# Sliding the operand window of a down projection: one row tile per visit in a ring of eight, and another order at the start of the up stage

## The chip, the cores and the metric

The kernel runs on one core of one Trainium2 chip. The metric is the time of one execution in microseconds on the device; lower is better. Before the change three runs took 2235.82, 2242.28 and 2243.55 us, median 2242.28 us.

## The reference

One layer of a decoder with two token groups, 512 prompt tokens and 8 x 4 sample tokens, 544 in all. A mixer (retention and sliding-window attention) comes first; then the feed-forward part, which is what the change touches:

```
def conv_ffn(h, conv_buf, ffn_norm_w, w_up, conv_w, conv_b, w_down):
    hn = rmsnorm(h, ffn_norm_w)
    up = jnp.einsum('btd,df->btf', hn, w_up)          # 2048 -> 2 x 5632
    g, u = jnp.split(up, 2, axis=-1)
    gp = jnp.concatenate([conv_buf.astype(g.dtype), g], axis=1)
    gc = conv_b + sum(gp[:, j:j + T] * conv_w[j] for j in range(CONV_W))
    y = jnp.einsum('btf,fd->btd', jax.nn.silu(gc) * u, w_down)   # 5632 -> 2048
    return y, gp[:, -(CONV_W - 1):]
...
hp = hp + mixer_output(ro, rg, so, ret_gn_w[l], w_o[l], hp.dtype)
f, cbuf_p = conv_ffn(hp, zbuf, ffn_norm_w[l], w_up[l], conv_w[l], conv_b[l], w_down[l])
hp = hp + f
```

All inputs are float32.

## The kernel before

**Precision.** A float32 product is made of three matmuls of a reduced float32 type: each operand is split into `hi` (a rounded copy, written by ACT) and `lo` (the rest, a subtraction on DVE), and hi x lo, lo x hi and hi x hi are summed (`split`, L149).

**Tiling.** The 544 tokens are two halves of 272 columns (256 prompt, 16 sample tokens), index u. Up and down projection both work on 2 x 2 blocks (two halves of tokens, two halves of the other sides) with seven products in place of eight, named `b11 t1 t2 b21 t3 b22 t4` in the order in which `unit` (L1104) makes them. A product (`product`, L1092) takes a weight block, 128 columns by up to eight row tiles of 128 rows; ACT and DVE split it (`uhi`, `ulo`; three buffers each), and PE runs 3 matmuls of 128 x 272 for each row tile against the seven moving operands in `xop`: `X_hi/X_lo` for b11, t1 and t2, `A_hi/A_lo` for the others. Each of the seven has eight slots, one for each row tile. Some weight blocks are sums on DVE (`usum`, L1132, L1135, L1146, and in place L1142).

**Up stage.** 44 visits (`up_pair`, f = 0 to 43), each with the seven products at eight row tiles. Behind each come the norm factor, the convolution, the gate (`joined`, `conv`, `gated`), and for every second visit `blocks` (L1196), which makes the seven operands of the down projection for one of its 22 row tiles j and writes them to DRAM (`hx_keep[0..6]`, by DMAs that POOL issues).

**Down stage.** The 22 row tiles do not fit into the eight slots, so they are taken in three chunks, `chunks = ((0, 8), (8, 7), (15, 7))` (L1217). For every chunk there are eight visits (`down_pair`, mp = 0 to 7, 256 output columns each): 24 visits. Results of the first two chunks are added into `x1_keep` in DRAM (`keep_y`), those of the last are finished and written out (`finish_y`, `emit_y`). Before a chunk, all seven operands are filled again: `fill(c, name)` (L1219) reads all row tiles of the chunk from `hx_keep` into the `lo` slots (one DMA issued by POOL) and splits them in place, four row tiles at a time. The fill of a product's operand is written behind that product in the last visit before the chunk:

```
1276  unit(load, (y[:, 1, 0], y[:, 1, 1]), todo, joined, sign=-1.0, behind=fills(c + 1) if mp == 7 else {})
1281  todo = up_pair(f, todo, behind=fills(0) if f == FT - 1 else {})
```

**Start of the up stage.** The stage before it, the second part of the output projection (L1026 to L1042), makes x1 one column block at a time (i = 0 to 15), and `build_x` makes the operands from two of them. After it come the four splits of L1043 to L1045 into `A_hi/A_lo` slots 0 to 7 (operands b21 and t4), then the sum of squares is turned into the norm factor by a matmul (`rstd_ffn`, L1078), then `unit` of f = 0 loads its weights (`uraw`, 7 buffers: 3 in pool `ua`, 4 in pool `ub`). Pool `ua` lies where the pools of the output projection (`wp`: raw, whi, wlo; `tb1`: x1, sq2, t1k) were.

**Order.** A scheduling layer turns the written order into one instruction stream for each engine; an engine runs its stream in order, and semaphores hold an instruction until what it needs is done. Weights come by DMAs that SP issues, `hx_keep` and `x1_keep` by DMAs that POOL issues.

## Time and profile before

| | us |
|---|---|
| median of three runs | 2242.28 |
| profiled execution | 2239.99 |
| its span, first to last instruction | 2238.2 |
| PE busy in the span | 2176.6 (97%) |
| DVE busy | 1630.1 (73%) |
| ACT busy | 1010.7 (45%) |
| POOL busy | 291.9 (13%) |

The mean granted clock of TensorE over the span is 0.986 of full speed. A busy share is an average over stages: the up stage runs from about 760 to 1715 us, the down stage from there to the end. The times in rows below count from the span's start.

### The profile page before, as it was taken

Reading aid. Unit: us, or ns where it says so; the run is one execution under the profiler, and the core shown is the slowest. Engines: PE = TensorE matmul, PEld = TensorE weight load, DVE = VectorE, ACT = ScalarE, POOL = GpSimd, SP = SyncE. Lnnn points to the kernel's source line nnn. Section 1 sums busy time; section 2 is a strip of 40 time slices with the busy share of each in tenths; the row PEclk is TensorE's granted clock in tenths of the full one; section 3 lists DMA queues with packets and bytes.
Section 4 is the critical chain, followed back from the end, with each engine's and each line's share of the span. In section 5 each row is a group of like instructions: output and inputs, shape, how many; then the busy total and the mean of one; then the engine's idle time right before and its main releaser. Section 6 shows DMA issues by size and latency. Waiting matters only on the chain.

```text
span 2238.2 us, 42004 instructions
## 1 busy us (share of the span) xinstructions
PE 2176.6 (97%) x17159; PEld 2139.1 (96%) x17159; DVE 1630.1 (73%) x2457; ACT 1010.7 (45%) x1612; POOL 291.9 (13%) x463
## 2 busy tenths in 40 slices
PE   7999999999999799999999999999998999898998
PEld 7999999999999799999999999999998999898998
DVE  5555557875437778888888888888888767767775
ACT  5122235566215544444444444444445445445444
POOL 1000000000003212122122122122122101001000
PEclk8999999999999899999999999999998999999999
DMA  9333343324644343343443443434436656557553
GB/s 289 100 97 94 87 88 77 82 67 120 130 115 136 112 124 114 113 145 107 121 137 113 124 125 116 133 114 126 124 116 224 149 128 194 139 131 221 140 150 98
DMA packets 452656, 286.52 MB, mean 128 GB/s; under 512 B 46320, under 2 KB 430640, under 8 KB 452080
## 3 DMA queue, kind: packets, MB, share of 16 engines
q1 hardware_dynamic: 433376, 222.16, 36.6%
q0 software_dynamic: 19088, 61.68, 9.1%
q8 instruction: 134, 2.20, 0.4%
q14 instruction: 58, 0.48, 0.1%
HBM read 231.38 MB, written 47.67 MB: 125 GB/s over the span
## 4 chain that ended last, share of the span: by engine, by line
PE 64%; issue 18%; DVE 9%; DMA 6%; POOL 2%; ACT 1%; SPq 1%; DVEq 0%; POOLq 0%; ACTq 0%
PE acc L174 17%; PE acc L178 9%; PE bx L1100 7%; PE bx L1099 6%; PE bx L1102 6%; PE zy L1099 5%; PE zy L1100 5%; PE zy L1102 4%; DMA uraw<-in_w_up_dram 3%; DVE ulo L151 3%; DMA A_lo<-hx_keep 1%; POOL x_keep L1267 1%; DVE cv L1186 1%; DVE us L1191 1%; PE sm L686 1%
## 5 line engine op out<-in xcount | busy, mean ns | idle before, releaser
L151 DVE TENSOR_TENSOR ulo<-uraw,uhi 128x1024 fp32r<-128x1024 f32 (+1 forms) x272 | 322.1, 1188 | 87.3 <-ACT uhi L150 87.0
L150 ACT CAST uhi<-uraw 128x1024 fp32r<-128x1024 f32 (+1 forms) x272 | 278.2, 1023 | 108.6 <-issue 72.2
L150 ACT CAST uhi<-usum 128x1024 fp32r<-128x1024 f32 (+1 forms) x204 | 209.3, 1026 | 227.0 <-DVE usum L1135 123.4
L1100 PE MATMUL bx<-X_hi,ulo 128*128 128x272 f32 x1056 | 277.2, 294 | 11.6 <-DVE ulo L151 11.4
L174 PE MATMUL acc<-A_lo,whi 128*128 128x272 f32 x1344 | 286.2, 294 | 1.4 <-DVE A_lo L290 0.8
L1099 PE MATMUL bx<-X_lo,uhi 128*128 128x272 f32 x1056 | 275.2, 291 | 9.7 <-ACT uhi L150 9.7
L174 PE MATMUL acc<-A_hi,wlo 128*128 128x272 f32 x1344 | 280.6, 290 | 0.0
L151 DVE TENSOR_TENSOR ulo<-usum,uhi 128x1024 fp32r<-128x1024 f32 (+1 forms) x204 | 242.6, 1189 | 47.3 <-ACT uhi L150 47.3
L1099 PE MATMUL bx<-A_lo,uhi 128*128 128x272 f32 x1056 | 271.0, 289 | 4.7 <-ACT us L1122 2.2
L1099 PE MATMUL zy<-A_lo,uhi 128*128 128x272 f32 x1056 | 272.5, 290 | 1.3 <-ACT p L1124 0.5
L1100 PE MATMUL zy<-A_hi,ulo 128*128 128x272 f32 x1056 | 271.4, 289 | 0.6 <-DVE ulo L151 0.6
L1100 PE MATMUL bx<-A_hi,ulo 128*128 128x272 f32 x1056 | 270.1, 287 | 0.0
L150 ACT CAST whi<-raw 128x1024 fp32r<-128x1024 f32 x100 | 104.8, 1048 | 279.4 <-PE acc L178 234.2
L174 PEld LDWEIGHTS acc<-A_lo,whi 128*128 128x128 f32 x1344 | 211.8, 189 | 7.9 <-issue 4.2
L1100 PEld LDWEIGHTS bx<-X_hi,ulo 128*128 128x128 f32 x1056 | 202.3, 192 | 16.5 <-DVE ulo L151 16.2
L174 PEld LDWEIGHTS acc<-A_hi,wlo 128*128 128x128 f32 x1344 | 211.9, 189 | 0.8
L1099 PEld LDWEIGHTS bx<-X_lo,uhi 128*128 128x128 f32 x1056 | 201.9, 191 | 11.0 <-ACT uhi L150 10.9
L1099 PEld LDWEIGHTS bx<-A_lo,uhi 128*128 128x128 f32 x1056 | 199.2, 189 | 5.8 <-ACT us L1122 2.4
L1099 PEld LDWEIGHTS zy<-A_lo,uhi 128*128 128x128 f32 x1056 | 199.7, 189 | 2.5 <-ACT p L1124 1.1
L1100 PEld LDWEIGHTS zy<-A_hi,ulo 128*128 128x128 f32 x1056 | 199.6, 189 | 0.8 <-DVE ulo L151 0.8
L1100 PEld LDWEIGHTS bx<-A_hi,ulo 128*128 128x128 f32 x1056 | 198.9, 188 | 0.0
L178 PE MATMUL acc<-A_hi,whi 128*128 128x272 f32 x1344 | 187.6, 290 | 0.0
(437 smaller groups left out, 4256.6 us busy)
## 6 DMA issues: line engine op xcount, KB each, us to landing
uraw<-in_w_up_dram SPq DMA_DIRECT2D x176, 512.0 KB
uraw<-in_w_down_dram SPq DMA_DIRECT2D x64, 448.0 KB
raw<-in_w_in_dram SPq DMA_DIRECT2D x52, 512.0 KB
uraw<-in_w_down_dram SPq DMA_DIRECT2D x32, 512.0 KB
hx_keep<-us POOLq DMA_DIRECT2D x88, 136.0 KB, 2.0
hx_keep<-tt POOLq DMA_DIRECT2D x66, 136.0 KB, 4.8
x_keep<-us POOLq DMA_DIRECT2D x32, 272.0 KB, 5.1
raw<-in_w_in_dram SPq DMA_DIRECT2D x32, 256.0 KB
```

The costliest lines, as they stand in the source:

```text
L150: act.copy(out=hi, in_=src)
L151: eng.tensor_tensor(out=lo, in0=src, in1=hi.bitcast(F32), op=sub)
L174: pe.matmul(acc[:, u, :HC], lhsT=w, rhs=x[:, u, :], start=(first and i == 0 and w is wh), stop=False)
L178: pe.matmul(acc[:, u, :HC], lhsT=wh, rhs=xh[:, u, :], start=False, stop=(last and i == n - 1))
L686: pe.matmul(po[:, 256 * kv:256 * kv + 256], lhsT=vS[:, n if n == 0 else n - 1 + kb, kv, :], rhs=t[:, kb, :], start=(j == 0), stop=(j == le ...
L1099: pe.matmul(bank, lhsT=hi[:, k], rhs=xl[:, k], start=(first and k == 0), stop=False, skip_group_check=True)
L1100: pe.matmul(bank, lhsT=lo[:, k], rhs=xh[:, k], start=False, stop=False, skip_group_check=True)
L1102: pe.matmul(bank, lhsT=hi[:, k], rhs=xh[:, k], start=False, stop=(k == n - 1), skip_group_check=True)
L1186: dve.scalar_tensor_tensor(out=cva, in0=g[:, 0:560], scalar=w0[:, f:f + 1], in1=cva, op0=mult, op1=add)
L1191: dve.tensor_tensor(out=us, in0=us, in1=rstd_bc, op=mult)
L1267: sth(out=x1_keep[2 * mp + i], in_=y[:, i], accum_op=add)
```

## The change

The three chunks go. The down stage still has 24 visits, in three rounds of eight, but the range of row tiles that a visit takes now moves on by one tile from visit to visit: visit v uses tiles t0 = start + v % 8 up to t0 + n, with (start, n) = (0, 6), (6, 8), (14, 8), row tiles counted modulo 22. For each output column block the three rounds still cover all 22 tiles once. A tile t lies in slot t % 8 of each operand. In each visit each operand gets one new tile (`next_fills`): its DMA is written behind that product, its split ("convert") four products later, behind that product's own weight split. Before the first visit six tiles for each operand are filled (`first_fills`): DMAs behind the products of f = 43, the split of b11's operand behind f = 43, those of the six others in visit 0, one product ahead of their use. A visit's weight block has six or eight row tiles instead of eight or seven; a range that passes tile 21 takes two DMAs.

At the start of the up stage the weight block of f = 0's first product is loaded and split already in the output projection's last pass, in its pools; b11 of f = 0 is written ahead of the last four splits of x and ahead of the norm factor's matmul; pools `ua` and `ub` open later (behind b11 and behind t1's split). f = 0 thus loads that block twice, once for b11 and once for the sums.

The transposes for the convolution's last rows (`conv_rows`) are written two visits later, and may not stand ahead of the last matmul written before them.

The diff, cut to its core:

```diff
@@ -1026,6 +1026,8 @@
         acc = half_project(m, 1, A_hi[:, 0:8], A_lo[:, 0:8])
+        if i == KT - 1:
+            first_w = stage_half(cols_of(w_up[0], 0), 0)
...
@@ -1040,19 +1042,25 @@
-    for u in range(2):
-        for k in range(0, 8, 4):
-            split(A_hi[:, k:k + 4, u], A_lo[:, k:k + 4, u], C[:, k + 8:k + 12, u])
-    tst.close()
-    wst.close()
     ost.close()
...
+    def open_ua():
+        tst.close()
+        wst.close()
+        ua.append(ust.enter_context(tc.tile_pool(name="ua", bufs=1, reuse_waits="tile")))
+
+    def last_x():
+
+        for u in range(2):
+            for k in range(0, 8, 4):
+                split(A_hi[:, k:k + 4, u], A_lo[:, k:k + 4, u], C[:, k + 8:k + 12, u])
+        cst.close()
+        ub.append(ust2.enter_context(tc.tile_pool(name="ub", bufs=1, side="right", reuse_waits="tile")))
...
@@ -1072,14 +1080,15 @@
-            pe.matmul(pm[:, :HC], lhsT=onesD, rhs=ssq[:, u, :], start=True, stop=True)
+            with tc.issue_after(ups["mm"].ins):
+                pe.matmul(pm[:, :HC], lhsT=onesD, rhs=ssq[:, u, :], start=True, stop=True)
...
@@ -1089,19 +1098,28 @@
+            ups["split"] = split(hi, lo, w)
+        for part in between:
+            part()
+        n = hi.shape[1]
         xh, xl = xop[x]
         for ks in parts or (range(n),):
             for k in ks:
-                pe.matmul(bank, lhsT=hi[:, k], rhs=xl[:, k], start=(first and k == 0), stop=False, skip_group_check=True)
-                pe.matmul(bank, lhsT=lo[:, k], rhs=xh[:, k], start=False, stop=False, skip_group_check=True)
+                q = (at + k) % 8
+                pe.matmul(bank, lhsT=hi[:, k], rhs=xl[:, q], start=(first and k == 0), stop=False, skip_group_check=True)
+                pe.matmul(bank, lhsT=lo[:, k], rhs=xh[:, q], start=False, stop=False, skip_group_check=True)
...
@@ -1123,34 +1140,40 @@
-        a11, a21, a22 = load(0, 0), load(1, 0), load(1, 1)
-        prod(bx, a11, "b11", True, False)
+        if first_w is None:
+            a11, a21, a22 = load(0, 0), load(1, 0), load(1, 1)
+            prod(bx, a11, "b11", True)
+        else:
+            prod(bx, first_w, "b11", True)
+            open_ua()
+            a11, a21, a22 = load(0, 0), load(1, 0), load(1, 1)
...
@@ -1208,31 +1234,65 @@
-    chunks = ((0, 8), (8, 7), (15, 7))
-
-    def fill(c, name):
-        def go():
-            j0, n = chunks[c]
...
+    rounds = ((0, 6), (6, 8), (14, 8))
+    late = {}
+
+    def window(v):
+
+        t0, n = rounds[v // 8]
+        return t0 + v % 8, n
+
+    def fill(t, n, name):
+
+        hi, lo = (a[:, t % 8:t % 8 + n] for a in xop[name])
+        raw = lo.bitcast(F32)
+
+        def load():
+            sth(out=raw, in_=hx_keep[order7.index(name)][:, t % FJ:t % FJ + n])
+
+        def convert():
+
+            a, d = ups["split"]
+            with tc.issue_after(a.ins), tc.issue_after(d.ins):
+                for h in range(0, n, 4):
+                    p = slice(h, min(h + 4, n))
+                    if name == "t2":
...
+                    else:
+                        split(hi[:, p], lo[:, p], raw[:, p])
+        return load, convert
+
+    def first_fills():
+
+        steps = [fill(0, rounds[0][1], name) for name in order7]
+        now = {name: step[0] for name, step in zip(order7, steps)}
+        for i in range(1, 7):
+            late[0, order7[i - 1]] = [steps[i][1]]
+
+        def end():
+            steps[6][0]()
+            steps[0][1]()
+
+        now["t4"] = end
+        return now
+
+    def next_fills(v):
+
+        if v == 23:
+            return {}
+        now = {}
+        for i, name in enumerate(order7):
+            now[name], convert = fill(v + 6, 1, name)
+            late.setdefault((v + (i + 4) // 7, order7[(i + 4) % 7]), []).append(convert)
+        return now
...
@@ -1273,12 +1338,14 @@
-        unit(load, (y[:, 1, 0], y[:, 1, 1]), todo, joined, sign=-1.0, behind=fills(c + 1) if mp == 7 else {})
+        behind = next_fills(v)
+        within = {name: late.get((v, name), ()) for name in order7}
+        unit(load, (y[:, 1, 0], y[:, 1, 1]), todo, joined, sign=-1.0, behind=behind, within=within, at=t0)
...
     for f in range(FT):
-        todo = up_pair(f, todo, behind=fills(0) if f == FT - 1 else {})
+        todo = up_pair(f, todo, behind={"t1": last_x} if f == 0 else first_fills() if f == FT - 1 else {})
...
-    for c in range(len(chunks)):
-        for mp in range(8):
-            if c == 0 and 1 <= mp < 6:
-                todo[3] = [conv_rows(mp - 1)]
-            todo = down_pair(c, mp, todo)
+    for v in range(24):
+        if 2 <= v < 7:
+            todo[3] = [conv_rows(v - 2)]
+        todo = down_pair(v, todo)
```

In these pieces of the engines' streams rows are in order; `x4` counts equal instructions.

DVE where the up stage begins, before the change: the output projection's last splits, the norm factor (g, cv, rstd_bc) and f = 0's first products (ulo, usum).

```order
L1018 TENSOR_TENSOR t1k<-C 128x272
L151 TENSOR_TENSOR A_lo<-C,A_hi 128x4x272
L151 TENSOR_TENSOR X_lo<-t1k,X_hi 128x272
L1011 SCALAR_TENSOR_TENSOR X_lo<-C,X_hi 128x272
L151 TENSOR_TENSOR A_lo<-C,A_hi 128x272
L1023 TENSOR_TENSOR C<-C 128x272
L1083 TENSOR_SCALAR g<-sm 128x272 x2
L151 TENSOR_TENSOR A_lo<-C,A_hi 128x4x272
L151 TENSOR_TENSOR ulo<-uraw,uhi 128x1024
L195 SCALAR_TENSOR_TENSOR cv<-g,rstd_bc 128x544
L1132 TENSOR_TENSOR usum<-uraw 128x1024
```

The same place after the change:

```order
L1018 TENSOR_TENSOR t1k<-C 128x272
L151 TENSOR_TENSOR A_lo<-C,A_hi 128x4x272
L151 TENSOR_TENSOR X_lo<-t1k,X_hi 128x272
L1011 SCALAR_TENSOR_TENSOR X_lo<-C,X_hi 128x272
L151 TENSOR_TENSOR A_lo<-C,A_hi 128x272
L1023 TENSOR_TENSOR C<-C 128x272
L151 TENSOR_TENSOR A_lo<-C,A_hi 128x4x272
L1156 TENSOR_TENSOR usum<-uraw 128x1024
L1166 TENSOR_TENSOR uraw<-uraw 128x1024
L151 TENSOR_TENSOR ulo<-usum,uhi 128x1024
L151 TENSOR_TENSOR ulo<-uraw,uhi 128x1024
L1159 TENSOR_TENSOR usum<-usum,uraw 128x1024
```

b11's weight split and the norm factor are gone from this place; the first weight work is now the sum for t1 (L1156).

SP's stream at the same place before the change, with the semaphores that each DMA waits for (DMASW and DMAHW: DMAs issued by POOL and by SP):

```order
L950 DMA raw<-in_w_o_dram 128x8x128 [waits DMAHW7_49,DVE_49]
L165 DMA uraw<-in_w_up_dram 128x8x128 [waits DMAHW2_49,DMAHW0_49,DVE_49]
L165 DMA uraw<-in_w_up_dram 128x8x128 [waits DMAHW1_49,PE_49]
L165 DMA uraw<-in_w_up_dram 128x8x128
L165 DMA uraw<-in_w_up_dram 128x8x128 [waits DVE_49]
```

And after it:

```order
L950 DMA raw<-in_w_o_dram 128x8x128 [waits DMAHW7_49,DVE_49]
L165 DMA raw<-in_w_up_dram 128x8x128 [waits DMAHW0_49,DVE_49]
L165 DMA uraw<-in_w_up_dram 128x8x128 [waits DMASW4_49,DMASW3_49,DMASW5_49,DMASW2_49,DMASW6_49,DMASW1_49,DMASW7_49,DMASW0_49,DVE_49]
L165 DMA uraw<-in_w_up_dram 128x8x128 [waits DMAHW3_49,DMAHW2_49]
L165 DMA uraw<-in_w_up_dram 128x8x128 [waits Pool_49]
L165 DMA uraw<-in_w_up_dram 128x8x128 [waits DVE_49,PE_49]
```

The load of b11's block comes first and lies in `raw`. The first `uraw` load behind it now lies on tb1's tiles: its DMASW waits are the POOL DMAs that read x1, its DVE wait is X_lo<-t1k of the last `build_x`.

DVE at the first fill, before the change: f = 43's last weight splits (ulo), then fills of eight tiles, two instructions of four tiles for each operand.

```order
L1146 TENSOR_TENSOR usum<-usum,uraw 128x1024
L151 TENSOR_TENSOR ulo<-uraw,uhi 128x1024
L151 TENSOR_TENSOR X_lo<-X_lo,X_hi 128x1088 x2
L151 TENSOR_TENSOR ulo<-usum,uhi 128x1024
L151 TENSOR_TENSOR X_lo<-X_lo,X_hi 128x1088 x2
L151 TENSOR_TENSOR ulo<-uraw,uhi 128x1024
L1229 SCALAR_TENSOR_TENSOR X_lo<-X_lo,X_hi 128x1088 x2
L1145 TENSOR_TENSOR us<-us,p_19260 128x272
L151 TENSOR_TENSOR A_lo<-A_lo,A_hi 128x4x272 x2
```

The same place after the change:

```order
L1166 TENSOR_TENSOR uraw<-uraw 128x768
L151 TENSOR_TENSOR ulo<-uraw,uhi 128x1024
L151 TENSOR_TENSOR ulo<-usum,uhi 128x1024
L151 TENSOR_TENSOR ulo<-uraw,uhi 128x1024
L151 TENSOR_TENSOR X_lo<-X_lo,X_hi 128x1088
L151 TENSOR_TENSOR X_lo<-X_lo,X_hi 128x544
L1170 TENSOR_TENSOR us<-us,p_19296 128x272
L151 TENSOR_TENSOR ulo<-uraw,uhi 128x768
L151 TENSOR_TENSOR X_lo<-X_lo,X_hi 128x1088
L1197 TENSOR_TENSOR g<-zy,tu 128x512
```

f = 43's weight splits now stand ahead of all fills; from t1's fill on they stand between the splits of visit 0 (128x768, six tiles).

POOL in the middle of the down stage, before the change: sums into x1_keep for a whole chunk, then seven fills, then sums again.

```order
L1267 DMA x_keep<-us 128x544 x14
L1224 DMA X_lo<-hx_keep 128x1904 x3
L1224 DMA A_lo<-hx_keep 128x7x272 x4
L1267 DMA x_keep<-us 128x544 x16
```

After the change, one visit:

```order
L1332 DMA x_keep<-us 128x544
L1258 DMA X_lo<-hx_keep 128x272
L1332 DMA x_keep<-us 128x544
L1258 DMA X_lo<-hx_keep 128x272 x2
L1258 DMA A_lo<-hx_keep 128x272 x4
```

The two sums of a visit now stand among seven loads of one tile.

## Rows read from the trace of the kernel before

**Rows 1.** The page: busy time of each engine and its share of the span.

```profile
PE 2176.6 (97%) x17159; PEld 2139.1 (96%) x17159; DVE 1630.1 (73%) x2457; ACT 1010.7 (45%) x1612; POOL 291.9 (13%) x463
```

**Rows 2.** PE's waits from 700 us on: total us, times, longest.

```profile
PE bx L1100 <- DVE ulo L151: 11.4, 13, 4.9
PE bx L1099 <- ACT uhi L150: 9.7, 3, 5.5
```

**Rows 3.** Stretches: length, busy us of PE PEld DVE ACT POOL, PEclk, DMA share, GB/s.

```profile
900.00:1680.00 780.00, 776.22 (x6164) 772.83 (x6163) 663.35 (x829) 367.85 (x515) 162.89 (x278) 1.00 0.41 122
1700.42:1734.63 34.21, 24.77 (x154) 23.96 (x153) 30.63 (x32) 22.47 (x27) 7.23 (x11) 0.80 0.76 256
1745.00:1880.00 135.00, 134.98 (x1079) 134.70 (x1077) 92.09 (x86) 55.81 (x78) 12.21 (x15) 1.00 0.55 126
2100.00:2220.00 120.00, 119.97 (x957) 118.50 (x957) 84.93 (x91) 57.72 (x98) 9.53 (x13) 1.00 0.50 137
```

**Rows 4.** Timeline of PE at the three fills: start, us, instruction.

```profile
1700.42 0.29 PE L1099 MATMUL zy<-A_lo,uhi 128*128 128x272 f32 x1
...
1734.63 0.28 PE L1099 MATMUL bx<-X_lo,uhi 128*128 128x272 f32 x1
...
1894.67 1.16 PE L1102 MATMUL zy<-A_hi,uhi 128*128 128x272 f32 x8
...
1922.50 1.04 PE L1102 MATMUL zy<-A_hi,uhi 128*128 128x272 f32 x7
...
2051.43 1.04 PE L1102 MATMUL zy<-A_hi,uhi 128*128 128x272 f32 x7
...
2086.29 1.03 PE L1102 MATMUL bx<-A_hi,uhi 128*128 128x272 f32 x7
```

**Rows 5.** Timeline of PE where the up stage begins.

```profile
757.52 2.17 PE L178 MATMUL acc<-A_hi,whi 128*128 128x272 f32 x16
...
773.82 0.43 PE L1099 MATMUL bx<-X_lo,uhi 128*128 128x272 f32 x1
...
774.27 0.43 PE L1099 MATMUL bx<-X_lo,uhi 128*128 128x272 f32 x1
...
781.94 0.28 PE L1099 MATMUL bx<-X_lo,uhi 128*128 128x272 f32 x1
```

**Rows 6.** Timeline of DVE at the same place.

```profile
763.25 1.46 DVE L1017 TENSOR_TENSOR C<-C 128x272 f32<-128x272 f32 x1
...
766.54 0.43 DVE L151 TENSOR_TENSOR X_lo<-t1k,X_hi 128x272 fp32r<-128x272 f32 x1
...
769.25 1.29 DVE L151 TENSOR_TENSOR A_lo<-C,A_hi 128x1088 fp32r<-128x1088 f32 x1 [0.52 <-ACT A_hi L150]
```

**Rows 7.** DMA from 740 to 800 us in 40 slices of 1.5 us.

```profile
GB/s 0 0 142 182 211 0 174 12 11 0 180 6 0 19 241 324 298 3 0 0 0 199 329 290 290 275 15 21 291 37 34 254 298 125 4 256 89 5 0 0
```

**Rows 8.** DVE by form from 1740 us: count, busy us, mean ns, idle before.

```profile
L151 DVE TENSOR_TENSOR ulo<-uraw,uhi 128x1024 fp32r<-128x1024 f32 x29 | 35.2, 1222 | 12.4 <-ACT uhi L150 12.3
...
L1145 DVE TENSOR_TENSOR us<-us,p 128x272 f32<-128x272 f32 x24 | 10.6, 442 | 20.8 <-ACT us L1124 20.8
L151 DVE TENSOR_TENSOR A_lo<-A_lo,A_hi 128x1088 fp32r<-128x1088 f32 x8 | 10.3, 1289 | 3.4 <-ACT A_hi L150 3.2
```

**Rows 9.** Timeline of DVE at the first fill.

```profile
1693.67 1.22 DVE L1135 TENSOR_TENSOR usum<-usum,uraw 128x1024 f32<-128x1024 f32 x1
...
1700.28 1.21 DVE L151 TENSOR_TENSOR ulo<-uraw,uhi 128x1024 fp32r<-128x1024 f32 x1
```

**Rows 10.** Timeline of POOL, start of the up stage and first fill.

```profile
763.08 1.32 POOL L1042 TENSOR_TENSOR rstd_bc<-rstd_bc,sq 128x544 f32<-128x544 f32 x1 [0.56 <-ACT sq L1041]
...
1693.76 0.54 POOL L1224 DMA_DIRECT2D X_lo<-hx_keep  x1
```

**Rows 11.** DMA issues, 1690 to 1735 us: count, KB each, us to landing.

```profile
A_lo<-hx_keep POOLq DMA_DIRECT2D x4, 1088.0 KB, 10.4
...
hx_keep<-us POOLq DMA_DIRECT2D x3, 136.0 KB, 2.0
```

More of the change, by code (lines that the diff above doesn't have):

```diff
@@ L1090, in b44, with product @@
         return a.rearrange("p u (b t) -> p u b t", t=4)
-    def product(bank, w, x, first, last, parts=None):
-        n = w.shape[1]
-        hi, lo = new_hi()[:, :n], new_lo()[:, :n]
-        split(hi, lo, w)
+    def product(bank, w, x, first, parts=None, between=(), at=0):
+        if isinstance(w, tuple):
+            hi, lo = w
+        else:
+            hi, lo = new_hi()[:, :w.shape[1]], new_lo()[:, :w.shape[1]]
+            ups["split"] = split(hi, lo, w)
+        for part in between:
+            part()
+        n = hi.shape[1]
         xh, xl = xop[x]
@@ L1111, in prod @@
         def prod(*a):
-            product(*a, parts=parts)
+            product(*a, parts=parts, between=within.get(a[2], ()), at=at)
             if a[2] in behind:
@@ L1209, in blocks @@
             sth(out=hx_keep[1][:, j], in_=tt[:, 2])
-        unit(load_up(f), (us[:, 0], us[:, 1]), todo, joined, behind=behind, parts=None if f else (range(7), range(7, 8)))
+        unit(load_up(f), result, todo, joined, behind=behind, parts=None if f else (range(7), range(7, 8)), first_w=None if f else first_w)
         return {1: [conv], 6: [gated], 2: [blocks] if f % 2 else []}
@@ L1234, in fills @@
-    def fills(c):
-        return {name: fill(c, name) for name in order7} if c < len(chunks) else {}
+    FJ = FT // 2
+    rounds = ((0, 6), (6, 8), (14, 8))
[14 more added lines that the diff above has]
+                    if name == "t2":
+                        act.activation(out=hi[:, p], in_=raw[:, p], func=AF.Copy, scale=-1.0)
+                        dve.scalar_tensor_tensor(out=lo[:, p], in0=raw[:, p], scalar=-1.0, in1=hi[:, p].bitcast(F32), op0=mult, op1=sub)
+                    else:
+                        split(hi[:, p], lo[:, p], raw[:, p])
+        return load, convert
@@ L1249, in emit_y, with down_pair @@
         ld(out=y_sample.rearrange("b t d -> (b t) d")[:, 128 * m:128 * m + 128], in_=ys)
-    def down_pair(c, mp, todo):
-        j0, n = chunks[c]
-        last = c == len(chunks) - 1
+    def down_pair(v, todo):
+        t0, n = window(v)
+        mp = v % 8
+        last = v >= 16
         y = new_us()
@@ L1258, in load @@
             col = 128 * (2 * mp + i)
-            ld(out=raw, in_=wd[256 * j0:256 * (j0 + n), col:col + 128].rearrange("(j two p) c -> two p j c", two=2, p=128)[q])
+            j0 = t0 % FJ
+            for k0, k1 in ((0, min(n, FJ - j0)), (FJ - j0, n)):
+                if k0 < k1:
+                    j = (t0 + k0) % FJ
+                    ld(out=raw[:, k0:k1], in_=wd[256 * j:256 * (j + k1 - k0), col:col + 128].rearrange("(j two p) c -> two p j c", two=2, p=128)[q])
             return raw
```

61 lines of the change are left out of this document (27 added, 34 removed).

## The prediction

> **What bounds the kernel now.** I read the page first: PE is busy for 97% of the span [rows 1], so only the stretches in which it is not are worth looking at. The list of PE's waits after the attention part comes next; its two longest groups are matmuls that wait for DVE's or ACT's split of a weight block, each with few waits of up to 5 us [rows 2]. The timeline of PE says where: at the start of the up stage and at the three fills of the down stage's operands. Elsewhere PE is full: 776.2 of 780 us in the up stage, and all but 0.1 us in two stretches of the down stage [rows 3]. That also gives the yardstick: 776.22 us for 6164 matmuls is 0.126 us each, 3.02 us for a product of eight row tiles, 2.64 us for seven, 2.27 us for six.
>
> What each place loses, as time between two matmuls less the matmuls between them:
> - First fill [rows 4]: 1700.42 (f = 43's b21 begins) to 1734.63 (visit 0's t2 begins) is 34.2 us. Six products of eight tiles need 18.1 us and eight transposes about 1.1 us. Lost: 15.0 us. DVE is busy for 30.6 of these 34.2 us and the mean granted clock is 0.80 [rows 3], so this stretch goes at DVE's pace, and PE runs part of it at the lower of its two levels.
> - Second fill [rows 4]: 1894.67 to 1922.50 is 27.8 us. Between these rows lie 8 + 24 + 3 x 21 + 14 = 109 matmuls, 13.7 us. Lost: 14.1 us.
> - Third fill [rows 4]: 2051.43 to 2086.29 is 34.9 us; 7 + 7 x 21 + 14 = 168 matmuls, 21.1 us. Lost: 13.8 us.
> - Start of the up stage [rows 5]: 757.52 to 781.94 is 24.4 us; 64 matmuls (8.1 us) and four of the norm factor (0.5 us). Lost: 15.8 us.
>
> **Part 1: second and third fill.** In the new order no visit is followed by seven fills of seven or eight tiles; each of visits 0 to 22 gets seven of one tile. The matmuls stay the same: 7 products x 3 x 8 x 22 tiles = 3696. So these two losses go: -27.9 us.
>
> What comes back is the spread work. A one-tile split on DVE has the size of the addition that takes 0.44 us [rows 8]; seven make 3.1 us in a visit. A visit at eight tiles takes 21.1 us of PE, and DVE is busy 92.1 / 135.0 = 68% of it [rows 3], 14.4 us. With the new splits 17.5 us, 83%. In the first round (six tiles, 15.9 us) the eleven weight splits and sums shrink by a quarter of 1.22 us each [rows 8], 3.4 us: 14.4 - 3.4 + 3.1 = 14.1 us, 89%. In the third round DVE is at 84.9 / 120 = 71% now [rows 3], which comes to about 83%. The up stage bears 85% (663.35 / 780) and loses 3.8 us of PE in its 37 visits there, 0.1 us in each [rows 3]. So the cover is DVE's slack; it is thinnest in the first round, where six-tile products also give less time ahead. Bounds: 0 us (all hidden) to 12 us (half a microsecond in each of 24 visits); I take 3 us, near the up stage's row. If the cover were gone, 3.1 us in each visit would show, 71 us.
>
> Each new split waits at the head of ACT's stream for its load, and behind it stand the next weight splits. The load is written behind product i, but needs no more than that product's first matmul to be done, and its split stands behind the weight split of product i + 4, which ACT and DVE do one to two products ahead of PE. So there are about three products, 9 us at eight tiles, for a load of 136 KB. In the first round the slots are free two visits earlier. The trace has no such load; a write of 136 KB lands 2.0 us after its issue, a load of 1,088 KB in the crowd of the first fill after 10.4 us [rows 11]. I take 3 us, near the row of its own size: not late.
>
> POOL issues 168 loads where it issued 21, 147 more, at 0.54 us as in the row [rows 10] about 79 us over 24 visits, beside 13% busy [rows 1]. During such an issue at 1693.76 a DVE addition from 1693.67 took 1.22 us [rows 9, 10], its usual length [rows 8]: no price. POOL's own addition is another matter: while it runs from 763.08, a DVE instruction of 0.43 us takes 1.46 us [rows 6, 10]. The change adds no such addition. [...]
>
> **Part 2: first fill.** Six tiles instead of eight, behind f = 43's own splits instead of between them. So f = 43 now ends undisturbed: its b21 begins at 1700.42 and four products of 3.02 us end at 1712.5 [rows 4]. DVE is at t3's weight split at 1700.28 [rows 9]. Ahead of it now stands a sum of six tiles (0.92 us), then t3's, b22's and t4's splits (3 x 1.22 us) and b11's fill (1.29 us for four tiles [rows 8], half for two: 1.9 us), with some 0.6 us of waiting for a split buffer: b11's operand is ready at 1707.4, in time. From there DVE has to do, up to t4's split of visit 0: six fills (11.4 us), seven splits and four sums of six tiles at 0.92 us (10.1 us), what is left of f = 43 (an up visit's 663.35 / 37 = 17.9 us less eleven of 1.22 us: 4.5 us), and small things of visit 0 and of tile 6 (2.5 us): 28 us, a little less as instructions overlap, for products that need 15.9 us of PE. In DVE's stream the addition that takes t3's result stands ahead of b22's sum and split, so DVE waits there once for PE, some 2.5 us. Then 1707.4 + 28 + 2.5 = 1738, and t4's 3 us: visit 0 ends at 1741, against 1712.5 + 15.9 = 1728.4 without stalls. Lost 12.6 us instead of 15.0: -2.4 us. Bounds: all hidden, -15; worse by 3 if visit 1 suffers too.
>
> **Part 3: start of the up stage.** b11 of f = 0 needs only weights split early and X slots ready by 757.5, so it runs from 759.5 to 762.6 instead of from 772. But then PE needs t1's weights, the sum of two blocks. Their loads stand in SP's stream behind the first `uraw` load, which now waits for X_lo<-t1k of the last build_x, because it lies on t1k's place. That ends at 766.54 + 0.43 = 766.97 [rows 6]. In the trace four loads were released when the last A_lo split ended at 770.5 [rows 6] and moved from about 771.7 to 779 [rows 7]: 1.2 us to begin, 1.7 to 1.8 us each. So three loads from 766.97 on are in at 773.4. DVE then does the sum, another sum, and t1's `lo`: 773.4 + 3 x 1.14 = 776.8. PE has idled since 762.6, and in the trace the matmuls after such a gap come every 0.225 us (a pair in 0.45 us [rows 5]), the lower level. 24 of them take 5.4 us: t1 ends at 782.2, against 781.94 now [rows 5]. The norm factor's four matmuls (0.5 us) now come in between later instead of inside a gap. So what b11 gains is lost in a new wait for loads, and this part is worth about 0; bounds -4 (loads faster, PE back at the upper level early) and +2.
>
> **Sum**, against the profiled execution (2239.99 us, span 2238.2, which is 2.3 below the median of the runs): 2239.99 - 27.9 + 3 - 2.4 + 0 = 2212.7. I forecast **2213 us**, with a range of its own of 2204 to 2222.
>
> **Rivals.**
> 1. Both starts are hidden as well: the first fill loses little, the up stage gains 4. Then 2240 - 27.9 - 10 - 4 + 1 = 2199. For it: f = 43 is free of fills. Against: 28 us of DVE work for 15.9 us of PE. Chance 0.10.
> 2. DVE is too full: the first round at 89% stalls in many visits, and where stalls come close together the clock falls. At 0.8 us in each of 24 visits, 19 us: 2229; at 1.2 us nothing is gained. For it: 89% is above anything that the trace shows hidden. Against: 85% cost 0.1 us a visit. Chance 0.18.
> 3. Each POOL issue holds up DVE for its 0.54 us or more: 7 x 0.75 = 5 us a visit, and DVE would need 19 of 15.9 us in the first round and some 23 of 21 to 22 us in the others. That is 8 x 3.2 + 16 x 1 = 42 us more: 2252, slower than before. The row at 1693.7 speaks against it. Chance 0.03.
> 4. Slower: the one-tile loads land late. The load waits for its own product, its split for the load, three products on; so a product cannot come more often than every third of issue plus landing. That decides from 9 us on, and the gain is gone at about 9.9 us. At the crowd's 10.4 us and 1 us of issue it is 3.8 us for each of 7 x 15 products instead of 3.02: 82 us, 2295. For it: queue rows of 10 us. Against: those moved eight times the bytes in a burst. Chance 0.03.
>
> **How the numbers follow.** Forecast 0.66, rivals 0.10, 0.18, 0.03, 0.03. A measurement can tell about 0.5%, 11 us, from no change: faster means below 2231. That is the forecast, rival 1 and some 0.11 of rival 2: 0.87. The same: the rest of rival 2 and part of rival 3, 0.08. Slower: 0.05. The range for 8 in 10 is 2202 to 2228: the forecast's own, the near side of rival 1 and about half of rival 2.
>
> **What would show it.** Right: no stretch of the down stage behind visit 1 with PE below 9 tenths; granted clock 1.00 there; DVE at 83 to 90%; visit 0 still with waits for `ulo` and a lower clock, about 12 us lost; f = 0's t1 waiting for a sum that waits for `uraw` loads, t2 begun near 782. Wrong: waits of ACT for X_lo or A_lo from hx_keep in most visits (rival 4), DVE instructions longer while POOL issues (rival 3), or PE gaps of a microsecond in every visit of the first round (rival 2).

## The result and the profile after

The changed kernel takes 2214.52 us (median of four runs, 2213.37 to 2219.16) against 2242.23 us for the kernel before in the same comparison: a ratio of 0.9886, interval 0.9862 to 0.9910. The forecast was 2213 us. The profiled execution took 2215.06 us with a span of 2213.3 us, 24.9 us less than before.

The page's first part, to be set against [rows 1]:

```profile
PE 2166.3 (98%) x17159; PEld 2132.4 (96%) x17159; DVE 1650.1 (75%) x2590; ACT 1032.8 (47%) x1745; POOL 366.7 (17%) x610
```

The same 17159 matmuls; 133 more instructions on DVE and on ACT, 147 more on POOL. PE's waits from 700 us on, against [rows 2] (us in total, times, longest):

```profile
PE zy L1115 <- ACT uhi L150: 14.9, 2, 13.8
PE bx L1116 <- DVE ulo L151: 8.2, 12, 3.6
PE bx L1115 <- ACT uhi L150: 3.6, 2, 2.4
```

One wait of 13.8 us (where the up stage begins) and in visit 0 one of 3.6 and one of 2.4 us are the longest that are left. Stretches by the same columns as [rows 3]: the up stage, visit 0 (up to the last matmul of visit 1's b11, whose other 17 PE does between visit 0's), and the three rounds of the down stage without their ends:

```profile
900.00:1680.00 780.00, 776.30 (x6162) 773.40 (x6161) 661.62 (x827) 368.06 (x515) 161.02 (x275) 1.00 0.41 122
1714.87:1746.13 31.26, 23.00 (x145) 22.15 (x144) 26.57 (x37) 15.96 (x27) 13.93 (x25) 0.84 0.69 216
1760.71:1858.92 98.21, 97.60 (x776) 96.72 (x775) 82.13 (x121) 59.21 (x119) 25.73 (x40) 1.00 0.79 185
1858.92:2027.51 168.59, 168.59 (x1346) 168.59 (x1345) 132.85 (x162) 88.16 (x152) 43.89 (x72) 1.00 0.71 173
2048.58:2182.80 134.22, 134.22 (x1070) 132.87 (x1069) 106.97 (x132) 74.66 (x138) 31.71 (x54) 1.00 0.66 186
```

In the second and third round PE is busy to the last digit. In the first it loses 0.6 of 98.2 us. The stretch of visit 0 is the only one of the down stage with long waits: 31.3 us at a mean clock of 0.84. Its 143 matmuls of these two visits need 18.0 us, so 13.2 us are lost.

The new loads and splits, against [rows 8, 10, 11]. First DVE's two kinds of split from 1760 to 2200 us (count, busy us, mean ns, idle before), then POOL's issues in the same stretch, then the page's DMA part (count, KB each, median us to landing):

```profile
L151 DVE TENSOR_TENSOR ulo<-uraw,uhi 128x1024 fp32r<-128x1024 f32 x64 | 78.2, 1222 | 31.3 <-ACT uhi L150 31.2
...
L151 DVE TENSOR_TENSOR A_lo<-A_lo,A_hi 128x272 fp32r<-128x272 f32 x87 | 37.9, 435 | 0.0
```

```profile
L1258 POOL DMA_DIRECT2D A_lo<-hx_keep x76 | 40.9, 538 | 166.9 <-PE bx L1115 87.7 <-PE zy L1115 71.1 <-issue 8.2
```

```profile
A_lo<-hx_keep POOLq DMA_DIRECT2D x92, 136.0 KB, 3.3
...
X_lo<-hx_keep POOLq DMA_DIRECT2D x69, 136.0 KB, 4.1
```

The weight split is as long as before, a one-tile split never waits (0.0), and a load lands in 3 to 4 us.

**Where the time went.** I cut both spans at the same matmuls: the last `acc` group of the output projection, the first matmul of f = 1, of f = 43 and of visit 2, the end. These are the cuts of the kernel before that [rows 5] does not have (start, us, instruction):

```profile
797.60 0.29 PE L1099 MATMUL bx<-X_lo,uhi 128*128 128x272 f32 x1
...
1691.19 0.29 PE L1099 MATMUL bx<-X_lo,uhi 128*128 128x272 f32 x1
...
1771.73 0.29 PE L1099 MATMUL bx<-X_lo,uhi 128*128 128x272 f32 x1
```

And PE in the changed kernel, with the rows that answer to [rows 5] in between:

```profile
757.22 2.17 PE L178 MATMUL acc<-A_hi,whi 128*128 128x272 f32 x16
759.24 0.29 PE L1115 MATMUL bx<-X_lo,whi 128*128 128x272 f32 x1
...
776.18 0.59 PE L1115 MATMUL zy<-X_lo,uhi 128*128 128x272 f32 x1 [13.79 <-ACT uhi L150]
...
782.48 0.29 PE L1115 MATMUL bx<-X_lo,uhi 128*128 128x272 f32 x1
...
799.04 0.29 PE L1115 MATMUL bx<-X_lo,uhi 128*128 128x272 f32 x1
...
1693.79 0.29 PE L1115 MATMUL bx<-X_lo,uhi 128*128 128x272 f32 x1
...
1760.71 0.29 PE L1115 MATMUL bx<-X_lo,uhi 128*128 128x272 f32 x1
```

| stretch | before | after | change |
|---|---|---|---|
| up to the last `acc` group | 757.52 | 757.22 | -0.3 |
| from there to f = 1 | 40.08 | 41.82 | +1.7 |
| f = 1 to f = 43 | 893.59 | 894.75 | +1.2 |
| f = 43 to visit 2 | 80.54 | 66.92 | -13.6 |
| visit 2 to the end | 466.47 | 452.59 | -13.9 |

The last two hold unequal work. Visits 0 and 1 have six row tiles now, so 84 matmuls (10.5 us) and eight transposes (1.1 us) have moved from the fourth stretch into the fifth. An up visit takes 21.07 us without waits; so f = 43, two visits of eight tiles and the eight transposes are 64.3 us, and with two visits of six tiles it is 52.8 us. Lost in f = 43 to visit 2: 16.2 us before, 14.1 after, most of it in visit 0. The rest of the down stage is 13.9 + 11.6 = 25.5 us better. That is the second and the third fill. The +1.2 between f = 1 and f = 43 is no more than scatter: in other traces with the same code there it takes 891.1 to 895.9 us.

Visit 0 in more detail: DVE, ACT and POOL there, one fence each, in time order, and a stretch.

```profile
1722.86 0.96 DVE L1156 TENSOR_TENSOR usum<-uraw 128x768 f32<-128x768 f32 x1 [2.49 <-DMA uraw<-in_w_down_dram]
...
1736.00 0.44 DVE L1170 TENSOR_TENSOR us<-us,p 128x272 f32<-128x272 f32 x1 [1.67 <-ACT us L1141]
```

```profile
1735.58 0.40 ACT L1141 ACTIVATE us<-bx 128x272 f32<-128x272 f32 x1 [3.59 <-DMA hx_keep<-us]
```

```profile
1724.95 1.06 POOL L1258 DMA_DIRECT2D A_lo<-hx_keep  x2 [4.27 <-issue]
1726.00 1.59 POOL L1258 DMA_DIRECT2D X_lo<-hx_keep  x3
1729.49 0.54 POOL L1258 DMA_DIRECT2D A_lo<-hx_keep  x1 [1.89 <-PE zy L1115]
1730.02 1.08 POOL L1227 DMA_DIRECT2D hx_keep<-us  x2
```

```profile
1710.17:1742.40 32.23, 23.97 (x153) 23.12 (x153) 28.08 (x42) 19.16 (x31) 15.02 (x27) 0.84 0.75 243
```

The last row is the stretch from the end of b11's fill to the end of t4's weight split, by the columns of [rows 3]: DVE works for 28.1 of 32.2 us. In it DVE waits twice, 4.2 us together. First for the weights of visit 1's t1, whose addition stands ahead of visit 0's t2 in its stream. Then for ACT, which may write t3's result into the one `us` buffer only when f = 43's stores have read it. Those stores stand on POOL behind one-tile loads of visits 1 and 2; one of these waits for visit 0's b21 (the row at 1729.49).

### The profile page after: what moved, and what is told of

Read it like the earlier page. It is cut to its first block, busy times and chain, and to the rows that moved or that the text cites. A ratio compares the mean times of both kernels' runs of the same rounds, so it can differ in the third digit from the quotient of the medians.

```text
span 2213.3 us, 42716 instructions
## 1 busy us (share of the span) xinstructions
PE 2166.3 (98%) x17159; PEld 2132.4 (96%) x17159; DVE 1650.1 (75%) x2590; ACT 1032.8 (47%) x1745; POOL 366.7 (17%) x610
## 4 chain that ended last, share of the span: by engine, by line
PE 82%; DVE 8%; DMA 5%; issue 4%; ACT 1%; SPq 1%; POOL 0%; DVEq 0%; ACTq 0%; POOLq 0%
PE acc L174 18%; PE bx L1116 10%; PE bx L1118 9%; PE bx L1115 9%; PE acc L178 9%; PE zy L1116 7%; PE zy L1115 7%; PE zy L1118 7%; DMA uraw<-in_w_up_dram 3%; DVE ulo L151 3%; DVE cv L1210 1%; PE sm L686 1%; PE sm L703 1%; DMA raw<-in_w_in_dram 1%; DVE us L1216 1%
## 5 line engine op out<-in xcount | busy, mean ns | idle before, releaser
L1116 PE MATMUL bx<-X_hi,ulo 128*128 128x272 f32 x1048 | 272.5, 292 | 8.3 <-DVE ulo L151 8.2
```

What stands on the lines that cost most here:

```text
L1116: pe.matmul(bank, lhsT=lo[:, k], rhs=xh[:, q], start=False, stop=False, skip_group_check=True)
```

## The experiments

Stretches are compared within each trace, from one of the cuts above to another, since the time up to the last `acc` group came out between 751.7 and 759.0 us in runs with the same code there.

### The sliding range with the old beginning of the up stage

The hunks on `first_w`, `open_ua`, `last_x`, the pools and the norm factor's matmul are taken back, for example:

```diff
-        if i == KT - 1:
-            first_w = stage_half(cols_of(w_up[0], 0), 0)
...
+    for u in range(2):
+        for k in range(0, 8, 4):
+            split(A_hi[:, k:k + 4, u], A_lo[:, k:k + 4, u], C[:, k + 8:k + 12, u])
```

> The changed kernel with the beginning of the up stage as it was before the change (weights of b11 loaded behind the output projection, last four splits of x and the norm factor's matmuls ahead of b11). Theory (the sliding range makes the whole gain, the new beginning is worth nothing): f = 1 begins near 797.6 us as before the change instead of 799.0, and the total stays within 3 us of the changed kernel, 2211 to 2216. Rival (the new beginning hides part of the old 15.8 us): the total goes up by 4 us or more.

Measured: 2216.02 us, ratio to before 0.9886 (0.9872 to 0.9899), the changed kernel's own. From the last `acc` group to f = 1 it takes 40.07 us, as before (40.08), against 41.82 with the new beginning:

```profile
755.23 0.29 PE L178 MATMUL acc<-A_hi,whi 128*128 128x272 f32 x1
...
795.30 0.29 PE L1107 MATMUL bx<-X_lo,uhi 128*128 128x272 f32 x1
```

So the whole gain is the sliding range's. The new beginning costs 1.7 us in the changed kernel's trace; in the traces of the runs below that have the same beginning the stretch takes 41.3 to 43.3 us, so it costs 1.2 to 3.2.

### Weight blocks of f = 0 away from t1k

```diff
         ua.append(ust.enter_context(tc.tile_pool(name="ua", ...)))
+        for name, shape in (("us", [128, 2, 2, HC]), ("tu", [128, 2, HC]), ("p5", [128, HC]), ("g", [128, 562])):
+            ua[0].tile(shape, F32, name=name, tag=name, bufs=1)
```

> The changed kernel with the first tiles of pool ua taken by us, tu, p5 and g, so that the weight blocks of f = 0 lie where raw, whi and wlo were and not on t1k and x1. Theory (the load waits for X_lo<-t1k, 766.7 us, and t1 for the load): the first block can be loaded from about 750, the second from about 757.5, all are in by 763; t1's sum then stands only behind the last A_lo split in DVE's stream (770.2), so t1's first matmul comes near 772.5 instead of 776.2 and t2 near 779 instead of 782.5; total 3 to 4 us less. Rival (the loads are not what t1 waits for, or they are slow wherever they lie): t1 stays at 776, total unchanged.

In the changed kernel SP issues the first block when X_lo<-t1k is done, as the semaphores said. SP's row, and the DVE rows before and after the loads:

```profile
766.70 25.50 SPq L165 DMA_DIRECT2D uraw<-in_w_up_dram  x11
```

```profile
766.24 0.43 DVE L151 TENSOR_TENSOR X_lo<-t1k,X_hi 128x272 fp32r<-128x272 f32 x1
...
773.83 1.23 DVE L1156 TENSOR_TENSOR usum<-uraw 128x1024 f32<-128x1024 f32 x1 [3.64 <-DMA uraw<-in_w_up_dram]
```

With the blocks elsewhere, t1's first matmul comes 15.2 us behind the last `acc` group (751.66) instead of 19.0:

```profile
766.88 0.59 PE L1117 MATMUL zy<-X_lo,uhi 128*128 128x272 f32 x1 [10.06 <-ACT uhi L150]
```

That is the 3.7 us expected at t1. Up to f = 1 only 1.8 us of it are left (40.0 us), and the total, 2213.10 us (2204.13 to 2217.36), cannot be told from the changed kernel's, so the 3 to 4 us expected there are not shown. The chain was read rightly; the wait has moved on in part, since PE now stops 1.9 us at t2 for DVE's split of the next sum.

### Weights of t1 and t2 in the output projection's pool too

```diff
-            first_w = stage_half(cols_of(w_up[0], 0), 0)
+            r11, r21, r22 = wraw(), wraw(), wraw()
+            for r, i2, q in ((r11, 0, 0), (r21, 1, 0), (r22, 1, 1)):
+                cols_of(w_up[0], DFF * i2)(r, q)
+            first_w = [whalf(), whalf()]
+            split(*first_w[0], r11)
+            dve.tensor_tensor(out=r21, in0=r21, in1=r22, op=add)
+            split(*first_w[1], r21)
...
+    def t2_w():
+        dve.tensor_tensor(out=r11, in0=r11, in1=r21, op=add)
```

> The changed kernel with the weights of t1 and t2 of f = 0, not only b11's, loaded, summed and split in the output projection's pool; the four blocks that f = 0 still needs are loaded again behind them. Theory (PE idles there only for t1's and t2's weights): t1 follows b11 at 762, t2 starts near 767.5 when its last operand tile is split, b21 near 771 behind the A_lo split; f = 1 begins 8 to 12 us sooner than 799.0, total 2203 to 2207. Rival (the wait only moves on to b21 and t3, whose blocks still lie on t1k and x1 or on C): f = 1 begins less than 5 us sooner, total 2210 or more.

```profile
766.14 0.39 PE L1130 MATMUL zy<-X_lo,whi 128*128 128x272 f32 x1 [2.38 <-DVE X_lo L151]
...
771.28 0.39 PE L1130 MATMUL zy<-A_lo,uhi 128*128 128x272 f32 x1 [1.42 <-ACT uhi L150]
```

In the place of the 13.8 us wait stand one for the last operand tile of t1 (2.4 us) and one for b21 (1.4 us); the longest of the others up to f = 1 is 1.9 us. f = 1 begins 33.8 us behind the last `acc` group, 8.0 less; the total is 2207.38 us (2203 to 2207 expected), ratio to before 0.9848 (0.9835 to 0.9862). What the new beginning was short of is the other two products' weights.

### The addition for visit 1 behind visit 0's t3

```diff
-        dve.tensor_tensor(out=s1, in0=a21, in1=a22, op=add)
+        if ups.get("v") == 1:
+            with tc.issue_after(ups["t3"][1].ins):
+                dve.tensor_tensor(out=s1, in0=a21, in1=a22, op=add)
```

> The changed kernel with the addition for visit 1's t1 held behind the weight split of visit 0's t3. In the changed kernel it stands ahead of the weight split of visit 0's t2 on DVE and waits there 2.5 us for its load. Theory (DVE's order, with the crowd of fill loads, stops PE at t2): DVE's wait and PE's 3.6 us wait go, visit 1 begins near 1743 instead of 1746.1, total 2 to 4 us less. Rival (the prediction's own: DVE has 28 us of work there for 15.9 us of PE, and what it saves at one place it pays at the next): visit 1 begins within 1 us of 1746.

f = 43 to visit 2 takes 67.4 us: no gain, 2213.54 us in all. DVE's first wait is gone, and its second has grown from 1.7 to 3.1 us:

```profile
1732.10 0.44 DVE L1174 TENSOR_TENSOR us<-us,p 128x272 f32<-128x272 f32 x1 [3.09 <-ACT us L1141]
```

```profile
ACT us L1141 <- DMA hx_keep<-us: 5.0, 1, 5.0
```

My expectation was wrong here: the stores set that second wait (ACT's wait for one has grown from 3.6 to 5.0 us), and DVE only reached it sooner.

### One-tile loads held behind f = 43's stores

```diff
-            sth(out=hx_keep[1][:, j], in_=tt[:, 2])
+            ups["stored"] = sth(out=hx_keep[1][:, j], in_=tt[:, 2])
...
+            with tc.issue_after(ups["stored"].ins) if held else ExitStack():
                 sth(out=raw, in_=hx_keep[order7.index(name)][:, t % FJ:t % FJ + n])
```

> The changed kernel with the one-tile loads written in visits 1 to 3 held, on POOL, behind the last store of f = 43 to hx_keep. In the changed kernel 11 of them stand ahead of those stores, one of them waits for visit 0's b21, and visit 0's t3 result waits on ACT 3.6 us for a store. Measure: from f = 43's first matmul to visit 2's, 66.9 us in the changed kernel (52.8 without stalls); the same code in three other runs took 67.4 to 68.7. Theory (POOL's order keeps the stores, these the us buffer, this ACT and PE): 63 to 65 us, total 2 to 5 us less. Rival of the prediction (DVE's 28 us of work set the pace whatever is late): 67 to 68 us, total unchanged.

62.7 us from f = 43 (1690.76) to visit 2 (1753.43), 4.2 less. The stretch differs from trace to trace: those with the same code in it have 66.9, 68.0, 68.4 and 68.7 us (the 67.4 named above is the run with the moved addition), so 4.2 us are beyond that scatter. The total, 2212.41 us (2205.10 to 2216.11), cannot be told from the changed kernel's. Of DVE's waits between 1708 and 1740 us one is left, and DVE is busy for 28.7 of 30 us where the changed kernel's has 25.9:

```profile
DVE usum L1156 <- DMA uraw<-in_w_down_dram: 1.3, 1, 1.3
```

```profile
1708.00:1738.00 30.00, 23.66 (x169) 22.59 (x168) 28.70 (x42) 19.46 (x32) 12.14 (x23) 0.94 0.68 215
```

### Two us buffers

```diff
-    new_raw = ring("uraw", [128, 8, 128], F32, 3, 4)
+    new_raw = ring("uraw", [128, 8, 128], F32, 3, 3)
-    new_us = ring("us", [128, 2, 2, HC], F32, 1, 0)
+    new_us = ring("us", [128, 2, 2, HC], F32, 1, 1)
```

> The changed kernel with two us buffers instead of one, paid for with one of seven uraw buffers. Visit 0's t3 result then needs no store of f = 43 to be done. Same measure, f = 43's to visit 2's first matmul. Theory (the us buffer is the link between POOL's late stores and PE): ACT's 3.6 us wait goes, 63 to 65 us; elsewhere nothing or a little is lost to the missing uraw buffer. Rival (DVE's amount of work, or weight loads that are late in the crowd): 66 to 69 us.

62.9 us from f = 43 to visit 2, and 2206.86 us in all. But most of the gain lies elsewhere. In the up stage PE is now busy without a gap, where the changed kernel loses 3.7 of 780 us. From f = 1 to f = 43 it takes 885.2 us instead of 894.8: 5.2 us of PE's idle time are gone, and the same 7058 matmuls are busy for 885.2 us instead of 889.5. So the short waits cost more here than the gaps that they leave in PE's row (9.5 us against 5.2). Up to f = 43 it is 10 us:

```profile
830.00:1680.00 850.00, 850.00 (x6779) 850.00 (x6778) 729.14 (x908) 410.77 (x564) 176.46 (x301) 1.00 0.41 123
```

In the changed kernel DVE waits there, 40 times between 842 and 1693 us, for a block of the next visit (44.8 us together); in this one it does not. The order of DVE's stream came out otherwise with the other rings, and I have not separated which of the two did it. The missing uraw buffer costs in visits 2 to 7, where DVE waits for weights (7.0 us in the changed kernel):

```profile
DVE usum L1156 <- DMA uraw<-in_w_down_dram: 17.7, 6, 3.8
```

From f = 43 to the end of the first round this kernel takes 168.9 us, the changed one 165.1.

### Without the first loads, and with short first splits

```diff
-        now = {name: step[0] for name, step in zip(order7, steps)}
+        now = {}
```

> The changed kernel without the seven loads of six tiles ahead of visit 0 (the splits stay and work on what lies there; the rest is as it was). 5.7 MB less between 1695 and 1728 us. Same measure. Theory (the crowd of transfers delays weight blocks and stores, DVE's work is only part of it): 58 to 62 us. Rival (DVE's work alone): 66 to 68 us as with the loads.

```diff
-                    p = slice(h, min(h + 4, n))
+                    p = slice(h, min(h + 4, n) if n == 1 else h + 1)
```

> The changed kernel in which each first split of six tiles works on two of them only (first of each group of four; the rest of the operand stays unsplit), so that DVE has about 7.5 us less to do between 1708 and 1741 us and ACT about 6; the loads stay. Same measure. Theory (transfers and POOL's order set the pace): 65 to 67 us. Rival (DVE's work sets it): 59 to 61 us.

Both kernels are one run each (2210.22 and 2212.99 us) and stand for this stretch alone. Without the loads f = 43 to visit 2 takes 62.8 us (1690.73 to 1753.54). That is between what the two theories said. The row for 1708 to 1738 us:

```profile
1708.00:1738.00 30.00, 23.89 (x168) 22.60 (x168) 29.22 (x43) 19.43 (x32) 11.67 (x21) 0.94 0.47 141
```

With 5.7 MB less to move DVE is busy for 29.2 of 30 us and waits for nothing but 0.6 us: so its amount of work seems enough to keep PE back by the 10 us that are left (62.8 less 52.8). The other 4.1 us of the changed kernel match DVE's two waits (4.2 us), and holding the loads or a second us buffer, which leave DVE's work as it is, gave them back as well.

The short splits gave 66.3 us, near what I wrote, but not for that reason: with less to do, DVE's stream came out with visit 1's addition still further ahead, and it waits there for 10 us. So this run does not measure DVE's work, and that the 10 us are DVE's work rests on its busy share in these traces alone.

```profile
1720.42 0.96 DVE L1156 TENSOR_TENSOR usum<-uraw 128x768 f32<-128x768 f32 x1 [10.04 <-DMA uraw<-in_w_down_dram]
```

### More work on DVE in every visit

```diff
+                    if n == 1:
+                        for q in range(2):
+                            h2 = hi[:, 0, 136 * q:136 * q + 136].bitcast(F32)
+                            dve.tensor_tensor(out=ups["x"], in0=h2, in1=h2, op=sub)
```

> The changed kernel with two additions of 128 x 136 on DVE behind each one-tile split, into a tile that nobody reads: 14 of about 0.22 us, 3 us more of DVE in each of visits 0 to 22. DVE is busy for 84% in the first round, 78% in the second, 77% in the third; with 3 us more this is about 102%, 92% and 91%. Theory (the spread splits are paid from DVE's slack, and cost nothing until it is used up): the second and third round lose under 4 us together, the first some 1 us a visit; total 4 to 12 us more. Rival (the prediction's rival 2: a share near 90% already stalls PE in every visit): 15 us more or above.

2232.20 us, 18 more than the changed kernel, so my expectation was wrong, and the rival had its number but not its mechanism. Three stretches, one in each round:

```profile
1775.00:1860.00 85.00, 85.00 (x683) 84.83 (x682) 84.97 (x181) 52.78 (x106) 21.29 (x33) 1.00 0.79 186
1870.00:2040.00 170.00, 169.65 (x1354) 169.38 (x1354) 158.04 (x276) 88.73 (x154) 44.87 (x73) 1.00 0.69 171
2060.00:2200.00 140.00, 130.71 (x1003) 128.14 (x1002) 113.60 (x200) 69.05 (x130) 49.25 (x50) 0.96 0.58 165
```

In the first round DVE runs without a gap (84.97 of 85.00 us), and PE does too; in the second DVE has 93% and PE loses 0.4 us of 170. Most of the loss is in the third, where DVE has less to do (81%): its visits take 22.3 to 29.5 us instead of 22.4. What is different there is a copy on POOL for the results that go out. In the changed kernel 14 copies take 780 ns on the mean and none more than 1.14 us; here, from 2050 to 2200 us, 12 of them:

```profile
L1305 POOL COPY tt<-us 128x32 f32<-128x32 f32 x12 | 29.8, 2484 | 25.4 <-PE sm L1309 15.3 <-DVE us L1342 10.0
```

```profile
2129.84 0.54 POOL L1258 DMA_DIRECT2D X_lo<-hx_keep  x1 [0.56 <-DVE ulo L151]
2133.57 5.95 POOL L1305 COPY tt<-us 128x32 f32<-128x32 f32 x1 [3.19 <-PE sm L1309]
2139.46 0.54 POOL L1258 DMA_DIRECT2D A_lo<-hx_keep  x1
```

From 2128.5 to 2139.8 us DVE's instructions follow one another without a gap, and the copy that starts at 2133.57 ends where they end (POOL's spans are rough). It is not the only one: seven copies take 3.6 us or more, and each ends within 0.3 us of the next gap of DVE that is at least 0.3 us long. In the changed kernel the copies that lie in such a gap take 0.21 us; but six there, of 1.07 us each, end 2.1 us ahead of the next one, so a copy can also end beside a busy DVE. That DVE holds the long copies up rests on the seven ends; no run changes the copies alone. Behind a copy on POOL stand the one-tile loads, and PE waits 8.4 us for the copies themselves:

```profile
PE sm L1309 <- POOL tt L1305: 8.4, 3, 4.0
```

### A distance of two products instead of four

```diff
-            late.setdefault((v + (i + 4) // 7, order7[(i + 4) % 7]), []).append(convert)
+            late.setdefault((v + (i + 2) // 7, order7[(i + 2) % 7]), []).append(convert)
```

> The changed kernel with the split of a one-tile load written two products behind its load instead of four. The loads land 3.3 and 4.1 us (median) after their issue, a product takes 2.3 to 3.0 us, and ACT works one to two products ahead of PE. Theory (three products of room hide the landing, one doesn't): ACT waits for loads in most products with uhi casts behind them, PE loses 0.2 to 1 us in many of 154 products, total 20 to 100 us more. Rival (the scheduler's own lead or the ring's spare slots leave room): under 5 us more.

2250.74 us, ratio to before 1.0041 (1.0021 to 1.0060): 0.4% slower than the kernel before. The first round is as in the changed kernel (visits of 16.0 to 16.7 us), since slots are free two visits ahead there. In the second a visit takes 22.1 to 24.8 instead of 21.1 us, in the third 24.0 to 27.2 instead of 22.4. ACT's waits from 1765 us on show the loads:

```profile
ACT A_hi L150 <- DMA A_lo<-hx_keep: 81.8, 45, 5.4
...
ACT X_hi L150 <- DMA X_lo<-hx_keep: 34.7, 23, 3.9
```

In the changed kernel neither line is there.

### The convolution's last rows later, in the kernel before

```diff
-            if c == 0 and 1 <= mp < 6:
-                todo[3] = [conv_rows(mp - 1)]
+            if c == 0 and 2 <= mp < 7:
+                todo[3] = [conv_rows(mp - 2)]
```

(with `issue_after` at the transposes, as in the change)

> The kernel before, with the transposes for the convolution's last rows alone moved as in the change: two visits later and not ahead of the matmuls written before them. In the kernel before PE waits 5.2 us for POOL (co) with two of them in visit 0, in the first fill's stretch. Measure: f = 43's to visit 2's first matmul, 80.5 us in the kernel before. Theory (the fills set that stretch, and PE would have waited for them anyway): 79 to 81 us, total unchanged. Rival (PE's in-order wait was part of the loss that the change removes): 75 to 77 us, total 4 to 5 us less.

2242.83 us, ratio 1.0007 (0.9994 to 1.0021); 79.6 us from f = 43 to visit 2, 0.9 less. PE's 5.2 us wait for POOL was time in which it would have waited for the fills.

### All together

Weights of three products early, loads held, two us buffers.

> The changed kernel with three edits of the runs so far together: weights of t1 and t2 of f = 0 in the output projection's pool (8.0 us less up to f = 1), one-tile loads of visits 1 to 3 held behind f = 43's stores (4.2 us less up to visit 2), two us buffers for one uraw buffer (4.1 us less up to visit 2, some 10 us less in the up stage, some 8 us more in visits 2 to 7). Theory: the first and the third add up, the second overlaps with the third: 2214.5 - 8.0 - 7.6 = 2199, between 2197 and 2202. Rival (the gains share one cause, PE's slack at the start of the up stage): 2204 to 2207.

2205.26 us (2202.54 to 2209.95), ratio to before 0.9845 (0.9822 to 0.9867). It is the fastest median here, but it cannot be told from 2206.86 and 2207.38. My 2197 to 2202 were too low; the number lies in the rival's 2204 to 2207. The rows don't show the rival's shared cause, though. Up to f = 43 this kernel is 16.0 us ahead of the changed one, of the 8.0 and 10.0 that the two edits gave alone; from f = 43 to the end of the first round it is 3.9 us behind, as the two-buffer run was (3.8). What is missing lies between the last `acc` group and f = 1, which takes 36.5 us here and 33.8 with the early weights alone. PE's waits there are the same in both traces (2.4, 1.9, 1.9 and 0.9 us); the granted clock is not, 0.86 here and 0.95 there:

```profile
757.12:793.59 36.47, 29.46 (x191) 28.23 (x189) 28.07 (x36) 20.26 (x28) 4.21 (x7) 0.86 0.57 160
```

```profile
755.96:789.75 33.79, 26.76 (x191) 25.49 (x189) 27.92 (x36) 20.09 (x28) 4.20 (x6) 0.95 0.69 188
```

The first row is this kernel's, the second that of the run with the early weights. Why the clock differs at equal waits stays open.

## Why the prediction was right, step by step

In the profiled executions 27.3 us less were forecast and 24.9 measured: 25.5 us less at the second and third fill, 2.1 less at the first, 1.7 and 1.2 us more in the up stage, 0.3 less ahead of it. The forecast started from a profiled run that was 2.2 us below its kernel's median, so that 2213 lies within 1.5 us of the median of 2214.52 is in part luck.

- **Second and third fill gone, -27.9.** Right. Net of the spread work the rest of the down stage is 25.5 us better; -27.9 + 3 was said.
- **Spread work +3.** A little less: visits 2 to 7 lose about 1 us together and the later rounds nothing. The 0.1 us for each visit of the up stage, from which the 3 us were taken, counted PE's idle time alone; the run with two us buffers shows 9.5 us in 42 visits, twice as much. DVE's share came out at 84, 79 and 80% where I had 89, 83 and 83%: a one-tile split takes 435 ns by itself, but in a full stream the next instruction starts 350 ns after it (1738.10 and 1738.45, for example).
- **Loads in time.** Right: they land 3.3 and 4.1 us after their issue, and ACT never waits for one. The run with a distance of two shows the edge that rival 4 described, and it is near: at half the distance the visits of the second and third round lose 1 to 5 us each.
- **POOL's issues hold nothing up (rival 3).** Right: 133 of them in the stretch from 1760 to 2200 us, 538 and 578 ns each, beside DVE instructions of 1222 ns, the length of [rows 8]. That an issue costs DVE 0.75 us, as the rival's sum has it, no run shows.
- **First fill, lost 12.6 instead of 15.0, DVE-bound.** The difference was right (-2.1 measured on my cuts, -2.4 said). The cause was right, as far as DVE's busy share shows it, for 10 of the 14 us: DVE's work, 28.1 us where 28 was said. The step that failed is "DVE waits there once for PE, some 2.5 us": it waits twice, 4.2 us, for a transfer in the crowd and, by way of ACT, for stores behind loads on POOL. That miss is small beside the 28 us, so the sum came out. I had asked whether the loads would be late for their splits, and not what they stand in front of in POOL's stream.
- **Start of the up stage, 0.** t2 begins at 782.48 us (782.2 said), for the reason given: the load waits for X_lo<-t1k. The matmuls of t1 come at the lower clock that was expected: 0.50 from 778 to 780 us, 0.225 us from one to the next. Up to f = 1 it is 1.7 us worse, inside the bounds (up to +2); in other traces with the same beginning it is up to 3.2.
- **Rival 2** (DVE too full at 89%) was priced on a wrong idea: in the run with more work on DVE, PE stayed full in the first round beside a DVE with no gap at all. The clock was 1.00 in that run's first two stretches and 0.96 in the third, in which PE loses 9.3 of 140 us.

The two levels of the clock of which the prediction speaks are 1.00 and 0.50: of 8820 stretches of 0.25 us from 0 to 2205 us in the trace of the kernel before, 8577 have 1.00, 223 have 0.50, and 20 lie between. Three stretches there by the columns of [rows 3], PE busy throughout each (11 matmuls in 2 us, or 18):

```profile
774.00:776.00 2.00, 2.00 (x11) 2.00 (x10) 1.88 (x3) 0.08 (x1) 1.10 (x2) 0.50 1.21 293
780.00:782.00 2.00, 2.00 (x18) 2.00 (x16) 2.00 (x3) 1.05 (x1) 0.00 (x0) 1.00 0.06 16
1714.00:1716.00 2.00, 2.00 (x11) 2.00 (x11) 2.00 (x2) 1.83 (x2) 1.10 (x3) 0.50 1.06 343
```
